# Output projection in seven products, convolution norm inside attention, and the second norm's rows transposed once

## The chip, the cores and the metric

The kernel runs on one core of a Trainium2 chip. The metric is the device time of one execution in microseconds. A core has TensorE (PE in the profile; matmuls and transposes, accumulating in PSUM), VectorE (DVE), ScalarE (ACT), GpSimd (POOL) and SyncE (SP, which here only issues transfers). Each engine runs its own list of instructions in order and waits for the others through semaphores. PEld is the loading of weights into PE, which runs beside the matmuls.

## What is computed

One layer of a block over 1024 tokens of width 1024, in float32, cut to what matters here:

```
h = rms_norm(x, norm1_g);  a, gate, q, k, v = split(h @ w_in)
conv = silu(layer_norm(depthwise_conv31(a * sigmoid(gate)) + dw_bias, conv_ln_g, conv_ln_b))
attn = neighbourhood_attention(rms(q), rms(k), v, rpb)   # 8 heads, 8 x 16 windows on a 16 x 64 grid
x = x + concat(conv, attn) @ w_out                       # (1024 x 1024) @ (1024 x 1024)
h = rms_norm(x, norm2_g)
x = x + (silu(h @ w_gate) * (h @ w_up)) @ w_down         # width 2816
```

## The kernel before

Every float32 factor is split into a high part, rounded to the format in which PE is fast, and a low part, the remainder: ACT casts, then POOL or DVE subtracts (`split`, L103 to L108). A product is then three matmuls, high x high, high x low, low x high (`mac`, L110 to L114), each 128x128 by 128x512.

The program is written in the order in which each engine is to run; no scheduler moves it. Work beside the matmuls is put into a list, `woven`, of which `weave` runs one entry after each `mac` of a stage. Weights arrive in chunks of 128x1024: `want` lists them, `issue` has SP load the next one, `take` splits it, `take_parts` splits it in pieces. Long-lived and passing tiles of 128x1024 share one pool of 22 buffers (`G`), larger ones six of 128x4096 (`H`); PSUM has four banks `mm`, two `tp` and one double bank `cv`.

The stages: (1) the input projection, one tile of 24 matmuls after another (`project`, `glu_step`; each calls `step`), with the convolution's 31 taps on DVE, ACT and POOL behind it (DVE L319, POOL L345 into `pa`). (2) Attention, a loop over i to 33, one iteration for a block of queries and two heads: scores s (PE L615), exponentials (DVE L628 subtracts the maximum, ACT L630), a reciprocal (DVE L635) and a scaling on POOL (L637), six transposes p on PE (L646), copies (L651), and the product o with v (L662); iterations 16 to 31 have 384 columns, earlier ones 288. The position biases `tab` and the windows of v, `vw`, are loaded by SP. (3) The output projection: `proj` adds eight row blocks of `w_out` to one tile of 128 tokens and 512 columns, `pj` for the first half of the columns, `pk` for the second, and `resid` (L775) adds the input. Among these matmuls stand the convolution's layer norm (`conv_stats`: four transposes y, L728, statistics on DVE, L735, root on ACT, scaling) and its SiLU (`conv_silu`: four transposes z, L761). (4) Row norms (`norm2`, `norm2_out`, L867) and the left factors of the gate and up projection. That projection is already one of seven products of halves: A11, A12, A22 and four sums of halves, S1 to S4, as left factors. `t2_one` transposes the normed rows of the first four token tiles (8 groups of four transposes, L994); `s_T` transposes the sums and A22 (five operands, 20 groups, L963), after `s_sum` has formed them on the untransposed rows (L944). The right factors are halves of `w_gate` and `w_up` and four sums of them, formed by DVE (`t_sums`, L893), for 22 blocks of columns i; `prep` splits the next one. (5) The down projection, which the change leaves alone.

## Time and profile before

| | us |
|---|---|
| median of 3 runs | 1063.14 (1063.02 to 1063.66) |
| the profiled execution | 1064.03 |
| its span in the trace | 1062.2 |
| PE busy | 1045.4 (98%) |
| DVE busy | 699.8 (66%) |
| ACT busy | 443.7 (42%) |
| POOL busy | 397.3 (37%) |

The span is from the first to the last instruction of the profiled execution. Shares of busy time are means over stages that differ. Matmuls overlap in the pipeline, so that their pitch, from one start to the next, says what one costs, and not the length of a row.

### The profile page before, as it was taken

The numbers are of one execution on the slowest core, as the hardware profiler recorded it, in microseconds if no ns is written. First come the engines' busy times: TensorE is split into PE (matmuls) and PEld (weight loads), VectorE is DVE, ScalarE is ACT, GpSimd is POOL, SyncE is SP. The second block draws the span as 40 slices with busy tenths as digits, with TensorE's granted clock in tenths as the row PEclk, the third lists the DMA queues.
The fourth block names the chain that finished last, engine by engine and source line by source line (L and its number), as shares of the span: only waits on it lengthen the run. The fifth ranks groups of instructions, "written<-read, shape, count | busy, mean of one in ns | idle before, by whom it ended". The sixth has DMA issues, their size and how long they took to land.

```text
span 1062.2 us, 13969 instructions
## 1 busy us (share of the span) xinstructions
PE 1045.4 (98%) x5068; PEld 847.3 (80%) x5068; DVE 699.8 (66%) x1072; ACT 443.7 (42%) x874; POOL 397.3 (37%) x308
## 2 busy tenths in 40 slices
PE   7999999999999999999999999999999999999997
PEld 5788888776667888788888888888888888888886
DVE  6768998966765247666565564564655567858883
ACT  6456346626776334532323223332233344433441
POOL 0126568823542301444554544545454200002310
PEclk9999999999999999999999999999999999999999
DMA  9416681245504412032322222232132597634641
GB/s 333 164 47 225 217 257 36 75 161 154 165 34 161 136 80 99 21 129 77 136 91 104 109 99 95 104 129 100 70 131 78 194 322 276 209 99 132 205 127 43
DMA packets 68244, 144.05 MB, mean 136 GB/s; under 512 B 12496, under 2 KB 21200, under 8 KB 67536
## 3 DMA queue, kind: packets, MB, share of 16 engines
q1 hardware_dynamic: 66336, 139.95, 38.3%
q10 hardware_dynamic: 1840, 3.22, 0.9%
q8 instruction: 40, 0.66, 0.3%
q14 instruction: 28, 0.23, 0.1%
HBM read 103.99 MB, written 44.76 MB: 140 GB/s over the span
## 4 chain that ended last, share of the span: by engine, by line
PE 94%; DMA 2%; DVE 1%; ACT 1%; POOL 1%; issue 0%; SPq 0%; POOLq 0%; ACTq 0%
PE B L112 6%; PE B L114 6%; PE B L113 6%; PE A L112 4%; PE D L112 4%; PE D L114 4%; PE A L114 4%; PE D L113 4%; PE A L113 4%; PE z L113 3%; PE z L112 3%; PE z L114 3%; PE gl L114 3%; PE gl L112 3%; PE gl L113 3%; PE o L662 2%
## 5 line engine op out<-in xcount | busy, mean ns | idle before, releaser
L319 DVE SCALAR_TENSOR_TENSOR cv<-u,par,cv 128x1009 f32<-128x1009 f32 (+14 forms) x85 | 108.5, 1276 | 1.9
L345 POOL TENSOR_TENSOR pa<-pa,pr 128x1022 f32<-128x1022 f32 (+10 forms) x31 | 74.2, 2392 | 35.5 <-ACT pr L344 26.5
L104 ACT CAST op<-sr 128x512 fp32r<-128x512 f32 x77 | 47.7, 619 | 52.1 <-PE B2d L114 26.3
L108 DVE TENSOR_TENSOR op<-sr,op 128x512 fp32r<-128x512 f32 x77 | 57.1, 742 | 16.1 <-ACT op L104 16.0
L1037 DVE TENSOR_TENSOR g<-B,g 128x512 f32<-128x512 f32 x22 | 15.2, 691 | 79.0 <-PE B L114 79.0
L1209 POOL TENSOR_TENSOR ou<-ou,resm 128x512 f32<-128x512 f32 x8 | 12.2, 1530 | 144.0 <-DMA resm<-xd 142.1
L1046 ACT ACTIVATE D<-D 128x512 f32<-128x512 f32 x22 | 12.8, 582 | 113.1 <-DVE D L1045 113.1
L1032 DVE TENSOR_TENSOR u<-B,g 128x512 f32<-128x512 f32 x22 | 15.2, 691 | 62.1 <-PE B L114 62.1
L104 ACT CAST op<-wd 128x512 fp32r<-128x512 f32 x66 | 40.9, 620 | 30.7 <-DVE wd L1124 18.4
L637 POOL TENSOR_SCALAR e<-e,rs 128x288 f32<-128x288 f32 (+1 forms) x64 | 34.1, 545 | 50.2 <-DVE rs L635 42.9
L108 DVE TENSOR_TENSOR op<-wd,op 128x512 fp32r<-128x512 f32 x66 | 50.4, 764 | 1.8
L893 DVE TENSOR_TENSOR ts<-gu,ts 128x512 f32<-128x512 f32 x44 | 51.0, 1159 | 0.8
L1035 ACT ACTIVATE A<-A 128x512 f32<-128x512 f32 x20 | 11.6, 582 | 76.3 <-PE A L114 76.3
L630 ACT ACTIVATE e<-e,mx 128x288 f32<-128x288 f32 (+1 forms) x64 | 36.2, 569 | 2.0 <-DVE mx L628 2.0
L628 DVE CUSTOM_DVE_ANT_0 e<-s,tab 128x288 f32<-128x288 f32 (+1 forms) x64 | 30.1, 505 | 8.1 <-PE s L615 8.0
L344 ACT ACTIVATE pr<-u,par 128x1022 f32<-128x1022 f32 (+10 forms) x31 | 34.2, 1135 | 1.2 <-ACT vs L405 1.2
L893 DVE TENSOR_TENSOR ts<-gu 128x512 f32<-128x512 f32 x22 | 34.1, 1551 | 0.0
L646 PEld LDWEIGHTS p<-ident,e 128*96 128x96 f32 (+1 forms) x192 | 20.1, 133 | 15.2 <-issue 10.5
L944 POOL TENSOR_TENSOR xn<-xn,xn 128x512 f32<-128x512 f32 x4 | 6.9, 1732 | 57.3 <-DVE sn L944 57.3
L646 PE MATMUL p<-ident,e 128*96 128x128 f32 (+1 forms) x192 | 27.6, 280 | 0.7 <-DVE pT L651 0.6
L662 PE MATMUL o<-pT,vw 96*64 96x128 f32 (+1 forms) x384 | 28.0, 281 | 0.0
L615 PE MATMUL s<-kT,qT 64*128 64x288 f32 (+1 forms) x128 | 26.7, 495 | 0.0
(1039 smaller groups left out, 3449.6 us busy)
## 6 DMA issues: line engine op xcount, KB each, us to landing
gu<-in_gu SPq DMA_DIRECT2D x44, 512.0 KB
sr<-sd SPq DMA_DIRECT2D x77, 256.0 KB
sd<-sd SPq DMA_DIRECT2D x22, 512.0 KB
wd<-in_wd SPq DMA_DIRECT2D x44, 256.0 KB
sd<-g SPq DMA_DIRECT2D x33, 256.0 KB
x<-in_x SPq DMA_DIRECT2D x16, 512.0 KB
xd<-x SPq DMA_DIRECT2D x8, 512.0 KB
resm<-xd SPq DMA_DIRECT2D x16, 256.0 KB
```

Source lines behind the costliest of these rows:

```text
L104: act.copy(hi, src)
L108: eng.tensor_tensor(*[w[..., sl] for w in (lo, src, hi.bitcast(F32))], OP.subtract)
L112: pe.matmul(acc, lh, rh, start=start, stop=False, skip_group_check=True)
L113: pe.matmul(acc, lh, rl, start=False, stop=False, skip_group_check=True)
L114: pe.matmul(acc, ll, rh, start=False, stop=stop, skip_group_check=True)
L319: dve.scalar_tensor_tensor(acc[:, o], uc[:, i], dwk[:, c, t:t + 1], acc[:, o], OP.mult, OP.add)
L344: act.activation(pr[:, o], uc[:, i], AF.Copy, scale=dwk[:, c, t:t + 1])
L345: pool.tensor_tensor(pa[:, o], pa[:, o], pr[:, o], OP.add)
L630: act.activation(e[:, hh], e[:, hh], AF.Exp, bias=mx, scale=-1.0, accum_out=rs[:, hh:hh + 1])
L646: pe.transpose(pt[:m, g * P:(g + 1) * P], es[i][:, hh, g * m:(g + 1) * m], ident)
L662: pe.matmul(os_[s_][hh * HD:(hh + 1) * HD, hp], vw[cb, rh + g][:, c:c + HD], pTs[i][:, g, hh], start=g == 0, stop=g == 2)
L893: dve.tensor_tensor(o, l, r, OP.subtract)
```

## The change

Five edits go together.

1. The output projection becomes seven products of halves. Tokens are halved (tiles 0 to 3 and 4 to 7), so are the rows of `w_out` (attention, convolution) and its columns. Products n1, n7, n4, n6, n5, n2, n3 run in this order, each over four token tiles `cb` and four row blocks `c`; n7 goes on in the banks of n1, n5 in those of n6. The left factors are `a11` (attention of the second token half), the convolution's two halves `A22` and `A12`, and Q1 to Q4, sums kept in the tiles `diff` and `rowf`, which DVE forms as results leave PSUM (`evac_lo`, `conv_diff`) and ACT and POOL split (`q_split`). The right factors are B11, B21, B22 and four block sums P1 to P4. `read` and `put` add each result to the input's rows.
2. Block sums of weights are made in DRAM: P1 to P4 of `w_out` (`w4`) and of the first four blocks of gate and up (`g4`). SP copies a block to DRAM, then POOL issues a transfer that adds another to it. P2 is made from P1, P4 from P2. The eight steps of `g4`, a megabyte each, lie at eight of the first eleven calls of `step`; the sixteen of `w4`, half a megabyte each, at the later projections and inside attention.
3. The convolution's norm moves into attention: transposes, statistics and an ACT copy at every third iteration to i = 24, the reciprocal root by a few small DVE operations instead of ACT's root, the scaling of two tiles in each of i = 28 to 31, from SBUF to SBUF. Four weight chunks instead of two are split inside attention, one piece per iteration from i = 13 on.
4. The second norm's rows are transposed once (`turn`, 16 groups of four); the sums S1 to S4 are formed on the transposed tiles and split without PE.
5. The first four gate and up blocks take their sums from DRAM; their splits all run on POOL, and their products come in another order. Signs of the sums change for all blocks, with additions and subtractions swapped at the results.

The core of the diff:

```diff
+    def sum_steps(w, parts):
+        h = P // parts
+
+        def put_(n, m, i):
+            return lambda: nc.sync.dma_start(pw[w, n][i * h:i * h + h], block(w, m)[i * h:i * h + h])
+
+        def add(n, m, i):
+            return lambda: pool.dma_start(pw[w, n][i * h:i * h + h], block(w, m)[i * h:i * h + h], accum_op=OP.add,
+                                          max_dma_last_dim=2048)
+        both = range(parts)
+        head = [put_(n, "B12", i) for n in ("P1", "P3") for i in both]
+        head += [add(n, m, i) for n, m in (("P1", "B11"), ("P3", "B22")) for i in both]
+        tail = [f(n, m, i) for n, l, r in (("P2", "P1", "B22"), ("P4", "P2", "B21"))
+                for f, m in ((put_, l), (add, r)) for i in both]
+        head.insert(7, tail.pop(0)) if parts == 2 else None
+        return head + tail
...
+    for n in ("B11", "P3", "P4", "P2", "P1", "B21", "B22"):
+        for j in range(2):
+            want(block("w4", n)[64 * j:64 * j + 64].rearrange("r (h e) -> (r h) e", h=2), f"{n}{j}", wq_dst(n, j))
...
+        if n_steps[0] in (1, 2, 4, 5, 6, 8, 9, 11):
+            gate_steps.pop(0)()
...
+        if t % 2:
+            aside_sum()
...
     def value(t):
+        if t % 2 == 0 or t > 4:
+            aside_sum()
...
-        act.copy(at[cb][0][:, :, rh], os_[s_])
-
-    def evac_lo(s_, cs=slice(0, 4)):
+            if not rowf:
+                rowf.extend(G(f"rf{j}").rearrange("p (c b q) -> p c b q", c=2, b=4) for j in range(2))
+            for j in range(2):
+                act.copy(rowf[j][:, :, cb], os_[s_][:, 2 * j:2 * j + 2])
+        else:
+            a11[cb] = [w.rearrange("p (c q) -> p c q", c=4) for w in lr(G(f"a11{cb}", F32R))]
+            act.copy(a11[cb][0], os_[s_])
...
+            dve.tensor_tensor(diff[j][:, :, cb], os_[s_][:, cs], rowf[j][:, :, cb], OP.subtract)
...
+    LHS = {"n7": "Q3", "n4": "A22", "n6": "Q2", "n5": "Q1", "n2": "A12", "n3": "Q4"}
+    RHS = {"n1": "B11", "n7": "P3", "n4": "P4", "n6": "P2", "n5": "P1", "n2": "B21", "n3": "B22"}
+    CB = (0, 3, 1, 2)
...
+            mac(acc, lhs(p, c, cb), [w[:, o + c * 512:o + c * 512 + 512] for o in (0, 2048)],
+                start and c == 0, c == 3)
...
+    def conv_norm(t):
+        y = conv_T(t)
+        st6 = SM(f"bs{t}", 6)
         dve.bn_stats(st6, y)
-        dve.bn_aggr(mv, st6)
-        act.activation(sd, mv[:, 1:2], AF.Sqrt, bias=eps)
-        cs[t] = y, mv, sd
-        if 1 <= t <= 4:
-            conv_scale(t - 1)
-        if t >= 4:
-            conv_scale(t)
-
-    def conv_scale(t):
-        y, mv, sd = cs.pop(t)
-        r = SM(f"br{t}", 1)
-        dve.reciprocal(r, sd)
+        dve.bn_aggr(mvs[:, t], st6)
         if t % 2 == 0:
-            xx = G(f"xh{t}")
-            xh.extend([xx[:, :512], xx[:, 512:]])
-        if t >= 6:
-            dve.tensor_scalar(xh[t], y, mv[:, 0:1], r, op0=OP.subtract, op1=OP.mult)
-        else:
-            nb = SM(f"bb{t}", 1)
-            dve.scalar_tensor_tensor(nb, mv[:, 0:1], -1.0, r, OP.mult, OP.mult)
-            act.activation(xh[t], y, AF.Identity, bias=nb, scale=r)
+            xh.extend(lr(G(f"xh{t}")))
+        act.copy(xh[t], y)
...
+    def conv_scale(t, eng):
+        eng.tensor_scalar(xh[t], xh[t], mvs[:, t, 0:1], rc[:, t:t + 1], op0=OP.subtract, op1=OP.mult)
...
+    def read(p, cb):
+        acc = pb[cb]
+        if p == "n1":
+            put(4 + cb, 0, acc)
+            put(4 + cb, 1, acc, OP.subtract)
+        elif p == "n7":
+            put(cb, 1, acc, OP.subtract)
+            put(cb, 0, acc)
+        elif p in ("n4", "n6"):
+            put(cb, 0, acc, OP.add if p == "n4" else OP.subtract)
+        elif p == "n5":
+            put(cb, 1, acc)
+            put(4 + cb, 1, acc)
+            norm2(cb)
+        elif p == "n2":
+            put(4 + cb, 0, acc)
+        else:
+            put(4 + cb, 1, acc)
+            norm2(4 + cb)
...
+        if i in (13, 17, 21, 25):
+            take_parts(jobs, more=i < 21)
+        for _ in range({2: 1, 4: 1, 5: 2, 18: 1, 21: 1}.get(i, 0)):
+            aside_sum()
...
+        if i % 3 == 0 and i < 27:
+            conv_norm(i // 3 - 1)
+        if i == 25:
+            root = rsqrt(rc, mvs[:, :, 1], "rc")
+        if 25 <= i < 28:
+            next(root)
+        if 28 <= i < 32:
+            conv_scale(2 * i - 56, dve)
+            conv_scale(2 * i - 55, dve)
...
+        if jobs:
...
+    products = [(i, p) for k in (0, 2) for p in ("m1", "m2") for i in (k, k + 1)]
+    products += [(i, p) for k in (0, 2) for p in SRC for i in (k, k + 1)]
+    products += [(i, p) for i in range(4, FB) for p in ORDER]
...
+    def turn(t, j):
+        if not h2:
+            h2.extend(H(f"h2{w}", F32R).rearrange("p (k s) -> p k s", s=512) for w in range(2))
+        pt = (tp, mm)[j](f"t2{t}{j}")
+        for i in range(4):
+            kb = 4 * j + i
+            pe.transpose(pt[:, i * P:(i + 1) * P], xn[t][:, kb * P:(kb + 1) * P], ident)
...
+            act.copy(hi, p3)
+            act.copy(w, pt)
+            rest.append(lambda: dve.tensor_tensor(lo, p3, hi.bitcast(F32), OP.subtract))
...
+    def group(p, cbs=CB):
+        for cb in cbs:
+            more = p in ("n7", "n5")
+            if not more:
+                pb[cb] = mm(f"{p}{cb}")
+            proj(p, cb, pb[cb], start=not more)
+            read(p, cb)
...
+    weaves(12, s0=lambda: (weigh(31), evac_hi(7), evac_lo(7)), s1=QS("Q3", diff, 0, pool), s2=lambda: tails.pop()(), s3=lambda: read("n1", 0),
+           s4=QS("Q3", diff, 1, pool), s6=C(0, 1), s10=take)
+    group("n1", CB[1:])
...
+    weaves(16, s1=C(0, 2), s5=take, s9=C(0, 3), s13=QS("Q2", diff, 0, pool))
+    group("n7")
...
+           s7=U(1, 0), s8=U(1, 1), s9=[lo2, lo2, prep], s10=[U(2, 0), take], s11=U(2, 1), s12=[lo2, lo2], s13=prep)
+    group("n2")
+    weaves(16, s3=prep, s7=prep, s9=N(4), s12=U(4, 0), s13=[U(4, 1), N(7)], s15=SS(0, 1, 2))
+    group("n3")
```

Three places show where instructions moved. First POOL, where the taps of the convolution end (`pa3`) and attention begins (`e0`, `e1`: the scaling of exponentials). Before:

```order
L345 TENSOR_TENSOR pa3_1620<-pa3_1620,pr327_1959 128x1012
L637 TENSOR_SCALAR e0_2066<-e0_2066,rs0_2067 128x288 x2
L637 TENSOR_SCALAR e1_2109<-e1_2109,rs1_2110 128x288 x2
L637 TENSOR_SCALAR e2_2146<-e2_2146,rs2_2147 128x288 x2
L637 TENSOR_SCALAR e3_2171<-e3_2171,rs3_2172 128x288 x2
```

and in the change:

```order
L212 DMA w4P1_65<-in_w4 256x512
L372 TENSOR_TENSOR pa3_1638<-pa3_1638,pr326_1940 128x1013
L372 TENSOR_TENSOR pa3_1638<-pa3_1638,pr327_1981 128x1012
L212 DMA w4P3_67<-in_w4 256x512 x2
L676 TENSOR_SCALAR e0_2091<-e0_2091,rs0_2092 128x288 x2
L212 DMA w4P2_66<-in_w4 256x512
L676 TENSOR_SCALAR e1_2135<-e1_2135,rs1_2136 128x288 x2
L676 TENSOR_SCALAR e2_2173<-e2_2173,rs2_2174 128x288 x2
L212 DMA w4P2_66<-in_w4 256x512
```

Adding transfers for P1, P3 and P2 now stand between the taps and between the scalings; POOL runs them in this order.

Then DVE at iterations 27 to 29 of attention (`e28`, `e29`: maximum subtracted; `pT`: the copy of a transposed tile; `mx` the read of its maximum). Before:

```order
L651 COPY pT25_2972<-p25_2965 128x3x128
L674 TENSOR_TENSOR at11_2824<-o5_2851,at10_2823 128x2x128
L635 RECIPROCAL rs27_2975<-rs27_2975 128x2
L628 ISA e28_3007,mx280_3009<-s280_2991,tab11_2356 128x384
L628 ISA mx280_3009 128x1
L628 ISA e28_3007,mx281_3012<-s281_2993,tab11_2356 128x384
L628 ISA mx281_3012 128x1
L651 COPY pT26_3005<-p26_2998 128x3x128
L674 TENSOR_TENSOR at11_2824<-o5_2851,at10_2823 128x2x128
L635 RECIPROCAL rs28_3008<-rs28_3008 128x2
```

and in the change:

```order
L726 TENSOR_TENSOR a111_3095<-o5_2968,a111_3095 128x256
L727 TENSOR_TENSOR df0_2512<-o5_2968,rf0_2337 128x2x128
L674 RECIPROCAL rs27_3116<-rs27_3116 128x2
L667 ISA e28_3155,mx280_3157<-s280_3139,tab11_2404 128x384
L667 ISA mx280_3157 128x1
L667 ISA e28_3155,mx281_3160<-s281_3141,tab11_2404 128x384
L667 ISA mx281_3160 128x1
L690 COPY pT26_3153<-p26_3146 128x3x128
L835 TENSOR_SCALAR xh0_2215<-xh0_2215,par_93 128x512 x2
L726 TENSOR_TENSOR a111_3095<-o5_2968,a111_3095 128x256
L727 TENSOR_TENSOR df1_2513<-o5_2968,rf1_2338 128x2x128
L674 RECIPROCAL rs28_3156<-rs28_3156 128x2
```

Between the copy of `pT26` and the next reciprocal, which POOL's scaling waits for, there now stand two scalings of convolution tiles (L835) and a second subtraction per evacuation (L727).

Last POOL at the end of attention. Before:

```order
L637 TENSOR_SCALAR e31_3110<-e31_3110,rs31_3111 128x384 x2
L108 TENSOR_TENSOR wo00_3190<-wo00r_2790,wo00_3190 128x256 x4
L108 TENSOR_TENSOR wo00_3190<-wo02r_3058,wo00_3190 128x256 x4
L108 TENSOR_TENSOR wo14_3576<-wo14r_3196,wo14_3576 128x1024
L108 TENSOR_TENSOR wo14_3576<-wo16r_3257,wo14_3576 128x1024
```

and in the change:

```order
L676 TENSOR_SCALAR e31_3260<-e31_3260,rs31_3261 128x384 x2
L118 TENSOR_TENSOR Q3_3369<-df0_2512,Q3_3369 128x1024
L118 TENSOR_TENSOR Q3_3369<-df1_2513,Q3_3369 128x1024
L118 TENSOR_TENSOR wP4_3421<-P40r_3278,wP4_3421 128x1024
L118 TENSOR_TENSOR wP4_3421<-P41r_3306,wP4_3421 128x1024
L118 TENSOR_TENSOR Q2_3510<-df0_2512,Q2_3510 128x1024
```

Weight chunks (`wP4`) now alternate with splits of operands (`Q3`, `Q2`), which need the last results of attention.

More of the change, by code (lines that the diff above doesn't have):

```diff
@@ L8 @@
 F32R = mybir.dt.float32r
+I32 = mybir.dt.int32
 AF = mybir.ActivationFunctionType
@@ L165, in part @@
                 raws.pop(i)
-                issue()
+                if more:
+                    issue()
         pos[1] += 1
@@ L959, in s_T @@
-        two = kb == 2
-        pt = cv("sp") if two else tp("sq")
-        for j in range(1 + two):
-            for t in range(4):
-                pe.transpose(pt[:, j * 512 + t * P:j * 512 + (t + 1) * P],
-                             s_rows(n, t)[:, (kb + j) * P:(kb + j + 1) * P], ident)
-        if two and n != "S4":
-            split(*[w[:, kb:kb + 2].rearrange("p k s -> p (k s)") for w in sop[n, "all"]], pt, (dve,))
-        else:
-            for j in range(1 + two):
-                split(sop[n][0][kb + j], sop[n][1][kb + j], lr(pt)[j] if two else pt, (dve,))
@@ L971, in s_weave @@
-    def s_weave(n):
-        skip = lambda: None
-        parts = [lambda kb=kb: s_T(n, kb) for kb in range(3)]
-        woven.extend([skip, skip, skip, skip, parts[0], parts[1], prep, parts[2]] if n == "S2" else
-                     [parts[0], skip, parts[1], skip, parts[2]])
+            split(sop[n][0][t], sop[n][1][t], s4[t // 2][:, t % 2], (eng,))
+            return
+        if n not in sop:
+            q = H(n, F32R).rearrange("p (w k s) -> p w k s", w=2, s=512)
+            sop[n] = [[q[:, h, i] for i in range(HK)] for h in range(2)]
+            sop[n, "all"] = [q[:, h] for h in range(2)]
@@ new lines, in build @@
+    group("n4")
+    weaves(16, s0=C(1, 2), s2=take, s5=C(1, 3), s7=QS("Q1", rowf, 1, pool), s10=take, s13=QS("Q4", diff, 0, pool))
+    group("n6")
+    weaves(16, s1=take, s3=QS("Q4", diff, 1, pool), s6=take, s9=N(0), s13=N(3))
+    group("n5")
+    while pos[0] < len(chunks):
+        issue()
+    for _ in range(3):
+        next_raw()
+    weaves(16, s0=take, s1=[N(1), U(0, 0)], s2=U(0, 1), s3=[lo2, lo2], s4=U(3, 0), s5=[U(3, 1), N(2)], s6=[lo2, lo2],
+           s7=U(1, 0), s8=U(1, 1), s9=[lo2, lo2, prep], s10=[U(2, 0), take], s11=U(2, 1), s12=[lo2, lo2], s13=prep)
```

400 lines of the change are left out of this document (221 added, 179 removed).

## The prediction

> **What bounds the kernel now.** I read the page first: the engines' shares, the granted clock, the chain that ended last.
>
> ```profile
> span 1062.2 us, 13969 instructions
> ...
> PE 1045.4 (98%) x5068; PEld 847.3 (80%) x5068; DVE 699.8 (66%) x1072; ACT 443.7 (42%) x874; POOL 397.3 (37%) x308
> ...
> PEclk9999999999999999999999999999999999999999
> ...
> GB/s 333 164 47 225 217 257 36 75 161 154 165 34 161 136 80 99 21 129 77 136 91 104 109 99 95 104 129 100 70 131 78 194 322 276 209 99 132 205 127 43
> ...
> PE 94%; DMA 2%; DVE 1%; ACT 1%; POOL 1%; issue 0%; SPq 0%; POOLq 0%; ACTq 0%
> ```
>
> TensorE is busy 98% of the span, is 94% of the chain that ended last, and never loses its clock. Then TensorE's waits, the longest and the one that concerns the second norm:
>
> ```profile
> PE z L112 <- ACT wk0h L104: 6.9, 1, 6.9
> ...
> PE t L994 <- DVE xn L867: 0.6, 1, 0.6
> ```
>
> Only the first is long, and the change does not touch the start. So an instruction taken off TensorE is worth its pitch, unless another engine in that stage becomes late. Last, the busy time of PE, PEld, DVE, ACT and POOL in the stages concerned, with clock, DMA share and GB/s behind them:
>
> ```profile
> 35.00:60.00 25.00, 25.00 (x119) 20.68 (x118) 20.62 (x38) 10.79 (x18) 2.52 (x2) 1.00 0.12 44
> ...
> 160.00:216.00 56.00, 54.91 (x257) 44.86 (x256) 50.80 (x58) 35.48 (x53) 48.51 (x22) 1.00 0.16 55
> ...
> 274.00:310.00 36.00, 36.00 (x325) 22.90 (x326) 27.39 (x94) 28.92 (x87) 22.14 (x37) 1.00 0.24 82
> ...
> 310.00:390.00 80.00, 79.95 (x419) 64.62 (x420) 34.86 (x74) 35.24 (x60) 17.40 (x16) 1.00 0.36 125
> 390.00:465.00 75.00, 73.90 (x376) 60.16 (x375) 51.62 (x75) 35.75 (x64) 23.11 (x17) 1.00 0.17 64
> ```
>
> The second half of attention is 274 to 310 us, the output projection and second norm lie in 310 to 465 us.
>
> **Part 1, matmuls removed.** The output projection has 8 token tiles x 2 column halves x 8 row blocks x 3 = 384 matmuls of 128x512; seven products of 4 x 4 x 3 make 336. That is 48 fewer. Their pitch, and what four transposes cost between them:
>
> ```profile
> 342.58 0.60 PE L761 MATMUL z<-ident,xh 128*128 128x128 f32 x4
> 342.93 0.47 PE L112 MATMUL pj<-wo,cm 128*128 128x512 f32 x1
> ...
> 344.17 0.39 PE L114 MATMUL pj<-wo,cm 128*128 128x512 f32 x1
> 344.40 0.60 PE L761 MATMUL z<-ident,xh 128*128 128x128 f32 x4
> ```
> ```profile
> 357.15 0.39 PE L112 MATMUL pj<-wo,at 128*128 128x512 f32 x1
> ...
> 358.51 0.39 PE L112 MATMUL pj<-wo,at 128*128 128x512 f32 x1
> ```
>
> From 357.15 to 358.51 are six matmuls: 0.227 us each (the 0.39 us is one pipelined instruction's length). 48 x 0.227 = 10.9 us off.
>
> **Part 2, transposes removed.** From 342.58 to 344.40 lie four transposes and six matmuls: 1.82 - 6 x 0.227 = 0.46 us for a group of four. Before, the second norm's rows are transposed in 8 groups and the five sums of their halves in 20; now the rows once, in 16, and the sums are formed behind it. 12 x 0.46 = 5.5 us off. The 8 groups of the convolution's norm leave the projection for attention at the same price: zero on TensorE. PE's sum is 1062.2 - 10.9 - 5.5 = 1045.8 us.
>
> **Part 3, what attention takes on.** Here PE is full and the other engines nearly are. One of the wide iterations:
>
> ```profile
> 301.71 0.92 PE L615 MATMUL s<-kT,qT 64*128 64x384 f32 x4
> ...
> 302.55 0.88 PE L646 MATMUL p<-ident,e 128*128 128x128 f32 x6
> ...
> 302.77 0.17 DVE L635 RECIPROCAL rs<-rs 128x2 f32<-128x2 f32 x1 [0.31 <-ACT e L630]
> 302.89 0.56 DVE L628 CUSTOM_DVE_ANT_0 e<-s,tab 128x384 f32<-128x384 f32 x1
> 303.11 1.14 POOL L637 TENSOR_SCALAR e<-e,rs 128x384 f32<-128x384 f32 x2 [1.32 <-DVE rs L635]
> ...
> 303.38 0.09 DVE L628 DVE_READ_ACCUMULATOR2_ANT mx<- 128x1 f32 x1
> ...
> 303.52 0.48 ACT L651 COPY pT<-p 128x384 f32<-128x384 f32 x1 [0.78 <-PE p L646]
> ...
> 303.90 0.62 ACT L630 ACTIVATE e<-e,mx 128x384 f32<-128x384 f32 x1
> ...
> 304.17 0.59 PE L615 MATMUL s<-kT,qT 64*128 64x384 f32 x2
> ```
>
> The period is 304.17 - 301.71 = 2.46 us, so 36 us are some 14.6 iterations. The pieces added to 274 to 310, by the nearest rows:
>
> ```profile
> L735 DVE BATCH_NORM_STATS2 bs<-y 128x6 f32<-128x512 f32 x8 | 5.6, 695 | 2.4 <-PE y L728 2.4
> ...
> L752 DVE TENSOR_SCALAR xh<-y,bm,br 128x512 f32<-128x512 f32 x2 | 1.6, 810 | 0.1
> L736 DVE BATCH_NORM_AGGREGATE bm<-bs 128x2 f32<-128x6 f32 x8 | 1.5, 182 | 0.3
> ```
> ```profile
> L669 ACT CAST at<-o 128x512 fp32r<-128x512 f32 x8 | 4.6, 569 | 0.0
> ...
> L104 ACT CAST wo<-wo04r 128x256 fp32r<-128x256 f32 x4 | 1.6, 391 | 0.0
> ```
>
> DVE: about four statistics at 0.695 + 0.182 = 0.88 (3.5 us) and eight scalings, which in the trace stand only with a PSUM source, 0.81 each (6.5): 27.4 + 3.5 + 6.5 = 37.4 us of work in 36. ACT: four copies at 0.57 (2.3), some six more weight casts at 0.39 (2.3): 28.9 + 4.6 = 33.5, 93% of the window. POOL has 14 us free for six more splits.
>
> The eight scalings lie in the last four iterations, two in each, 1.6 us where DVE has 2.46 x (1 - 27.4 / 36) = 0.6 free: 1.0 us short four times over, of which the last one to two may run out under the projection's first matmuls. That bounds this piece between 0, if a scaling from SBUF to SBUF costs half of the PSUM row, and 4 us; I take 1.5. [...]
>
> Elsewhere in attention, iterations where a statistic, a conv copy and an evacuation meet are over 2.46 us on one engine while the mean is under it; besides, long-lived tiles take buffers from the pool that the exponentials use, so that from the sixteenth iteration on several of them wait until TensorE has read the tile of two iterations earlier. The loop behind such a wait is two score passes (1.3 us by the rows above), the exponential of the second part and its sum (0.62 + some 0.2), the reciprocal 0.17, the scaling on POOL 1.14 and p 0.88: 4.3 us of the 4.92 of two iterations. A statistic (0.88) in between makes it 5.2, 0.3 too many. At most about a third of the 16 wide iterations meets one: 0 to 2 us; I take 1. Four of POOL's accumulating transfers are issued here too; no POOL transfer stands in the trace, and the cheapest row next to it is a scaling held up by one POOL operation, 0.58: 0 to 2 us; I take 0.5. Attention: +3.0 us, between 0 and 8.
>
> **Part 4, the projection and second norm.** Before loses 75.0 - 73.9 = 1.1 us in 390 to 465, of which 0.6 is the row above, transposes that wait for normed rows. These go with their code: -1.1. Now TensorE waits where the order of products runs into an operand: the second product needs the first difference split on POOL.
>
> ```profile
> L108 POOL TENSOR_TENSOR wo<-wo14r,wo 128x1024 fp32r<-128x1024 f32 x1 | 2.4, 2418 | 23.9 <-ACT wo L104 23.9
> ```
> ```profile
> L775 DVE TENSOR_TENSOR x<-pj,x 128x512 f32<-128x512 f32 x8 | 5.1, 685 | 11.3 <-PE pj L114 11.3
> ```
>
> POOL has some 18 splits of 2.42 (8 of operands, 10 of weights), 44 us, in the 76 that 336 matmuls take; DVE 36 additions at 0.69 (25) and about 31 for the convolution and norms. Neither fills the stage, but the second product is due 36 matmuls, two groups of transposes and one o after the first full column of the first, 36 x 0.227 + 1.4 = 9.5 us, and its operand is ready after the last evacuation and the convolution result that enters it (some 3.5 us of DVE and ACT rows at 0.4 to 0.7) and two splits of 2.42: 8.4 us. At the end, the last two normed rows come within a microsecond of their transposes. Between 0 (all in time) and 4 us (both late by one 2.4 us split); I take 1.5, near the 1.1 of before.
>
> **Part 5, sums in DRAM.** Sixteen megabytes more are copied or accumulated, 8 MB for gate and up beside the input projection and 8 MB for the output weights later. The cover is the rows above: the DMA engines are 12% busy in 35 to 60 us and 16% in 160 to 216. POOL is 10% busy in 35 to 60, so that it can stand at a wait there. The later points:
>
> ```profile
> 89.19 0.39 SPq L141 DMA_DIRECT2D ag13r<-in_ag  x1
> ```
> ```profile
> 111.28 1.03 ACT L104 CAST ag13h<-ag13r 128x1024 fp32r<-128x1024 f32 x1
> ```
> ```profile
> 208.97 7.29 POOL L345 TENSOR_TENSOR pa<-pa,pr 128x1014 f32<-128x1014 f32 x3 [0.52 <-ACT pr L344]
> 231.38 0.99 POOL L637 TENSOR_SCALAR e<-e,rs 128x288 f32<-128x288 f32 x2 [15.11 <-DVE rs L635]
> ```
>
> SP waits for an accumulation before it copies its result, with weight loads queued behind; a load is issued 111.28 - 89.19 = 22 us before its use. POOL issues four adds among the last products of the taps, then idles 15.1 us. I cost it at 0; without cover it is rival C. The first four gate and up blocks save DVE its sums; POOL splits them all, one per product of 12 matmuls (2.7 us), half of the 2.42 each: 0.
>
> **Sum.** 1045.8 - 1.1 + 3.0 + 1.5 = 1049.2 us span. The profiled execution took 1064.03, 1.8 more than its span and 0.9 more than the runs' median: 1049.2 + 1.8 - 0.9 = 1050.1, said as 1050 us, 1.2% faster.
>
> **The rivals.** *B, attention becomes bound by its helpers.* If every one of the 16 wide iterations pays the 0.3 us of the buffer loop or the short queue of ACT (93% full, in order), and the four scalings their full 4 us: 1050 - 3 + 16 x 0.3 + 4 = 1056; at 0.5 each, 1059. For it: DVE's 37.4 of 36. Against: the narrow first half has room, and spare work spills past 310. *C, slower: the accumulating transfers are slow.* SP's copy of the second gate sum stands behind the add of the first, issued two steps of 24 matmuls (2 x 24 x 0.227 = 10.9 us) earlier; with the loads' 22 us of lead TensorE waits once one add takes over 33 us per MB, and the chain of sums has two such places. The gain of 13 us is used up at 33 + 6.5, some 40 us per MB; at 45 it is 1050 + 2 x 12 = 1074. Against: the page's GB/s row has 333 in its first slice, by which a megabyte that is read and written takes some 6 us. [...] *D, nothing is late:* 1045.8 - 1.1 + 0.9 = 1045.6, if scalings are cheap and the queues absorb the peaks. That the change does less than it says is excluded by the program: PE's order has 48 matmuls and 48 transposes fewer.
>
> **How the numbers follow.** The forecast 0.57, D 0.15, B 0.2, C 0.08. The range that holds 8 in 10 reaches from below D to B's upper case: 1044 to 1060, with the tails and C outside. About 0.2% (2 us) can be told from no change; faster 0.88, same 0.04 (a B with more stalls, or C near its threshold), slower 0.08.
>
> **What would show it.** Matmuls of the projection at 0.227 us each and 336 of them; 64 transposes of normed rows; wide iterations at 2.46 us except the last four; the scaling's row near 0.4 or 0.8; PE's waits in 310 to 450 under 2 us in all; POOL and SP with no long idle time before weight loads. A period of 2.8 or more from the sixteenth iteration on makes B right; PE waiting for a cast of `ag` or `w` rows before 216 us, or for `vw`, makes C right.

## The result: 1.4% slower

The changed kernel took 1079.1 us (median of four runs, 1076.97 to 1080.49); the kernel before, on the same chip, 1063.4 (1063.02 to 1065.1). The ratio is 1.0143, with a 95% interval from 1.012 to 1.0166. The prediction was 1050, 1044 to 1060: wrong in sign, and outside its range.

**The profile after**, the page first:

```profile
span 1075.1 us, 13899 instructions
...
PE 1035.1 (96%) x4972; PEld 837.7 (78%) x4972; DVE 720.7 (67%) x1097; ACT 463.7 (43%) x911; POOL 454.6 (42%) x342
...
PEclk9999999999979999999999999999999999999999
...
PE 77%; DMA 5%; SPq 5%; issue 4%; DVE 4%; POOL 3%; ACT 2%; POOLq 0%; DVEq 0%; ACTq 0%
```

The 96 instructions are gone from TensorE (5068 to 4972) and its busy time fell by 10.3 us, yet the span grew by 12.9. TensorE's idle time rose from 1062.2 - 1045.4 = 16.8 us to 1075.1 - 1035.1 = 40.0. The chain that ended last, 94% PE before, is now only 77%, with 10% on transfers and on the queue that issues them, and one slice of the clock has a 7. The prediction had 1049.2 us of span, of which 1045.4 - 16.4 = 1029.0 busy and 20.2 idle. So it missed 19.8 us of idle time and 6.1 us by which TensorE was busy longer.

Where the idle time is, by TensorE's waits:

```profile
PE p L685 <- POOL e L676: 12.3, 2, 11.9
PE z L122 <- ACT wk0h L114: 5.9, 1, 5.9
PE p L685 <- DVE pT L690: 3.7, 6, 1.1
PE z L123 <- POOL pa L367: 3.4, 1, 3.4
PE z L123 <- POOL w02l L118: 1.9, 1, 1.9
PE t L1065 <- DVE xn L961: 1.2, 1, 1.2
PE B L124 <- POOL t0m L118: 1.1, 1, 1.1
PE B L122 <- DVE u L1183: 0.8, 1, 0.8
```

The second row stood there before (6.9). The rest falls into three places: attention (12.3 and 3.7), the input projection (3.4 and 1.9), and the second norm with the product that follows (1.2, 1.1, 0.8). The windows show the first two, and what the stalls do to the clock (busy PE, PEld, DVE, ACT, POOL; granted clock; DMA share; GB/s):

```profile
116.00:160.00 44.00, 38.08 (x159) 30.53 (x158) 35.65 (x32) 15.95 (x17) 30.59 (x14) 0.96 0.78 237
274.00:310.00 36.00, 27.09 (x236) 17.03 (x236) 20.43 (x74) 21.35 (x64) 17.09 (x28) 0.94 0.62 176
302.00:314.00 12.00, 1.14 (x10) 0.35 (x6) 0.68 (x4) 0.74 (x3) 0.26 (x1) 0.65 0.65 204
330.00:343.00 13.00, 11.37 (x97) 7.45 (x94) 12.70 (x42) 8.85 (x28) 6.89 (x13) 1.00 0.18 56
```
```profile
155.40:158.80 3.40, 3.40 (x8) 2.72 (x9) 3.26 (x5) 0.89 (x2) 3.40 (x2) 0.50 0.81 210
...
315.10:319.20 4.10, 4.10 (x22) 2.73 (x22) 1.85 (x7) 3.06 (x11) 2.48 (x5) 0.50 0.00 0
466.00:469.40 3.40, 3.40 (x10) 2.63 (x9) 3.29 (x4) 2.09 (x4) 3.40 (x3) 0.50 0.43 110
```

The last three rows are stretches behind or beside waits in which TensorE works at a granted clock of 0.50; matmuls of 128x512 start 0.43 us apart there (155.95 to 158.51 us, six of them) and 0.23 at the full clock (469.60 to 470.97, six).

From 302 to 314 us **every** engine stands: PE is busy 1.14 us of 12, DVE 0.68, ACT 0.74, POOL 0.26. ACT's timeline and SP's list say why:

```profile
300.16 0.59 ACT L816 COPY xh<-y 128x512 f32<-128x512 f32 x1
313.26 0.40 ACT L114 CAST wP<-P30r 128x256 fp32r<-128x256 f32 x1 [12.51 <-DMA P30r<-w4P]
313.57 0.47 ACT L690 COPY pT<-p 128x384 f32<-128x384 f32 x1
313.94 0.62 ACT L669 ACTIVATE e<-e,mx 128x384 f32<-128x384 f32 x1
```
```profile
278.40 2.34 SPq L627 DMA_DIRECT2D tab<-tf  x1
280.84 9.42 SPq L639 DMA_DIRECT2D vw<-vd  x4
290.35 9.76 SPq L151 DMA_DIRECT2D P30r<-w4P  x1
```

ACT came to the first cast of P3's chunk (`P30r`) and waited 12.51 us for the load; the copy and the exponential behind it, which do not use that chunk, waited too, and with them TensorE. SP issued the load only at 290.35, behind window loads (`vw`) and a bias table, and the issuing instruction alone lasted 9.76 us. The chain has the whole flight in one row:

```profile
290.35 22.83 DMA P30r<-w4P
```

The kernel before had the same kind of load, in the same crowd, and far more slack:

```profile
L141 SPq DMA_DIRECT2D wo00r<-in_wo x1: 6832/6832/6832, 277.2 to 277.2; - x1
```
```profile
L104 ACT CAST wo<-wo00r x1: 1034/1034/1034, 319.5 to 319.5; 128x1024 fp32r<-128x1024 f32 x1
```

Its first use was at 319.5, 42 us after the issue. It was slow too: of the sixteen completions that the trace records for it, twelve come at 286.9 to 287.7 and the last four at 294.2 to 295.9, 18.7 us after the issue. Apart from bursts, two to three tenths of the DMA engines are busy until 296 us, with the window loads (40 slices of 0.65 us from 274 to 300 us, in tenths):

```profile
DMA  3222231322222222579522224999222220000000
```

By moving two weight chunks into attention, the change put a deadline at 300.75 (313.26 - 12.51) on a load that went out later.

In the input projection SP is again at the start of it. SP between 64 and 82 us, and its long wait there:

```profile
66.91 4.62 SPq L512 DMA_DIRECT2D t<-in_rpb  x6
76.42 0.53 SPq L209 DMA_DIRECT2D g4P<-g4P  x1
```
```profile
SPq L209 <- DMA g4P<-in_g: 4.8, 1, 4.8
```

The copy that starts gate's P4 stands 4.8 us for the add that finishes P2, and everything behind it on SP is later. What reaches TensorE is the load of `w02r`; in the kernel before and after:

```profile
133.45 0.53 SPq L141 DMA_DIRECT2D w02r<-in_qkv  x1
```
```profile
142.94 0.53 SPq L151 DMA_DIRECT2D w02r<-in_qkv  x1
```

It goes out 9.5 us later, and TensorE waits 3.4 + 1.9 us soon after.

The theories at this point: **Q**, queues: loads leave SP too late, in attention (P3) and in the input projection (gate sums), and the idle time and the lost clock follow; the sums of work in the prediction are right. **R**, bandwidth: sixteen megabytes more of traffic slow every load, whatever the order. **S**, a part of Q: the gate sums alone cause the stalls before 160 us.

### The profile page after: what moved, and what is told of

The parts are those of the page before. It is cut to its first block, busy times and chain, and to the rows that moved or that the text cites. A ratio compares the mean times of both kernels' runs of the same rounds, so it can differ in the third digit from the quotient of the medians.

```text
span 1075.1 us, 13899 instructions
## 1 busy us (share of the span) xinstructions
PE 1035.1 (96%) x4972; PEld 837.7 (78%) x4972; DVE 720.7 (67%) x1097; ACT 463.7 (43%) x911; POOL 454.6 (42%) x342
## 4 chain that ended last, share of the span: by engine, by line
PE 77%; DMA 5%; SPq 5%; issue 4%; DVE 4%; POOL 3%; ACT 2%; POOLq 0%; DVEq 0%; ACTq 0%
PE B L124 5%; PE B L122 5%; PE B L123 5%; PE D L124 4%; PE D L122 4%; PE D L123 4%; PE A L124 3%; PE A L122 3%; PE A L123 3%; PE z L123 3%; PE z L122 3%; PE z L124 3%; PE n L122 2%; PE n L124 2%; PE n L123 2%
## 5 line engine op out<-in xcount | busy, mean ns | idle before, releaser
L1200 ACT ACTIVATE D<-D 128x512 f32<-128x512 f32 x22 | 12.8, 582 | 116.7 <-DVE D L1199 116.7
L685 PE MATMUL p<-ident,e 128*96 128x128 f32 (+1 forms) x192 | 29.1, 285 | 16.5 <-POOL e L676 12.3
L987 DVE TENSOR_TENSOR ts<-ts,gu 128x512 f32<-128x512 f32 x36 | 43.3, 1202 | 0.6
L873 DVE TENSOR_TENSOR x<-x,n 128x512 f32<-128x512 f32 x40 | 26.0, 680 | 14.3 <-PE n L124 13.1
L690 DVE COPY pT<-p 96x384 f32<-96x384 f32 (+1 forms) x32 | 17.7, 552 | 19.0 <-ACT pT L690 18.7
L987 DVE TENSOR_TENSOR ts<-gu 128x512 f32<-128x512 f32 x18 | 30.1, 1671 | 0.0
## 6 DMA issues: line engine op xcount, KB each, us to landing
g4P<-in_g POOLq DMA_DIRECT2D x4, 1024.0 KB, 12.5
```

The costliest lines, as they stand in the source:

```text
L685: pe.transpose(pt[:m, g * P:(g + 1) * P], es[i][:, hh, g * m:(g + 1) * m], ident)
L987: dve.tensor_tensor(lr(tsum[i, 1])[n - 3] if o is None else o, l, r, OP.add)
```

## The experiments

Each edit is against the changed kernel. Quoted expectations call the theories by these letters.

**1. P3's first load ahead of the windows**

```diff
+        if i == 6:
+            issue()
         if i in (6, 12):
             load_window(i // 6)
         if i in (13, 17, 21, 25):
-            take_parts(jobs, more=i < 21)
+            take_parts(jobs, more=i == 17)
```

(`more` has `take_parts` issue the next load too.)

> The changed kernel with one transfer moved: the load of the first chunk of P3 is issued by SP ahead of the window loads of iteration 6, instead of behind those of iteration 12. Theory Q (order of the queue): that load stood behind eight window loads which move only some 100 GB/s, landed at 313 us, and ACT, whose list is in order, stood at its cast with the exponentials behind it. Then ACT's wait of 12.5 us and TensorE's of 11.9 us go, the clock stays at full speed in attention, and the time is 1079 - 12 - 2 = about 1065 us. Rival E (attention's engines are simply full): the wait moves to the next iterations and the time stays above 1074 us.

Measured: 1069.37 us (1067.94 to 1070.02), ratio to before 1.0058 (1.0041 to 1.0074), 9.7 us less than the changed kernel. The windows from 250 to 320 us, of the changed kernel and of this one:

```profile
250.00:320.00 70.00, 55.98 (x495) 37.39 (x496) 40.27 (x149) 43.92 (x133) 32.39 (x57) 0.90 0.58 168
```
```profile
250.00:320.00 70.00, 64.67 (x570) 42.92 (x570) 48.74 (x177) 51.04 (x154) 37.05 (x64) 0.98 0.63 182
```

The same bytes in another order give TensorE 8.7 us more work in this stretch, at a clock of 0.98 instead of 0.90, and ACT has no wait for `P30r`. That is Q; R, whatever the order, would have kept the wait. The time is 4 us above the expected 1065: the stage still loses 5.3 us, and DVE now waits 4.9 us for the bias table `tab`, which stands behind P3's load.

**2. Without the sums for P4 of the output projection** (P2's weights stand in for P4's, so the result of that product is another; two copies and two adds in DRAM fall away)

```diff
-            want(block("w4", n)[64 * j:64 * j + 64].rearrange("r (h e) -> (r h) e", h=2), f"{n}{j}", wq_dst(n, j))
+            want(block("w4", "P2" if n == "P4" else n)[64 * j:64 * j + 64].rearrange("r (h e) -> (r h) e", h=2), f"{n}{j}", wq_dst(n, j))
...
-        for _ in range({2: 1, 4: 1, 5: 2, 18: 1, 21: 1}.get(i, 0)):
+        for _ in range({2: 1, 4: 1}.get(i, 0)):
```

> The changed kernel without the four steps in DRAM that make the block sum P4 (two copies by SP at iteration 5, two accumulating transfers by POOL at iterations 18 and 21); the product n4 then uses P2, so this part of the output is left out. All loads stay in their places. Theory Q: SP gains the 3 us of the two copies and some more from less traffic, so P3's chunk lands a few us earlier, but most of the wait stays: ACT's wait 5 to 10 us instead of 12.5, time 1070 to 1076 us. Rival R (the accumulating transfers hold the load up): the wait falls under 2 us and the time to about 1065 us.

Measured: 1071.56 us, one run.

```profile
ACT wP L114 <- DMA P30r<-w4P: 7.7, 1, 7.7
```

The wait shrank from 12.5 to 7.7 us and did not go. SP did not come to the load earlier (at 293.05, in the changed kernel at 290.35); the flight became shorter, 15.3 us instead of 22.8:

```profile
293.05 15.31 DMA P30r<-w4P
```

POOL's two adds for P4, issued at 288.94 and 298.81 in the changed kernel, are what no longer runs beside it. So R has a share, 4.8 us of the wait; the 7.7 us that are left go when the load leaves ahead of the window loads (experiment 1). Leaving this traffic out brought 7.5 us by this one run, and reordering 9.7.

**3. Without gate's sums** (B11 stands in for P1 to P4 of gate and up's first four blocks; all eight steps fall away)

```diff
-        if n_steps[0] in (1, 2, 4, 5, 6, 8, 9, 11):
+        if n_steps[0] in ():
             gate_steps.pop(0)()
...
-                src = block("g4", SRC[n])[64 * j:64 * j + 64].rearrange("(i r) (h e) -> (r h) i e", i=2, h=4)
+                src = block("g4", "B22" if SRC[n] == "B22" else "B11")[64 * j:64 * j + 64].rearrange("(i r) (h e) -> (r h) i e", i=2, h=4)
```

> The changed kernel without the eight steps in DRAM that make the gate and up block sums beside the input projection; the first four blocks then use block B11 in place of P1 to P4, so that part of the output is left out. Theory S (SP's wait): SP stood 4.9 us for the second accumulating transfer and some 4 us more at slowed bias loads, and SP has no slack because it issues without pause from 66 to 165 us, so the loads of w01 to w03 came 9.5 us late. Then TensorE's waits of 5.8 us between 145 and 157 us go, and w02's load is issued at about 133.5 us instead of 142.9; time about 1079 - 6 - 2 = 1071 us. Rival P: POOL's order of splits is the cause; the waits stay above 4 us.

Measured: 1069.21 us, one run. The window that lost 5.9 us is full, and `w02r` leaves as early as it did in the kernel before:

```profile
116.00:160.00 44.00, 44.00 (x196) 36.44 (x195) 41.16 (x41) 19.23 (x21) 32.60 (x15) 1.00 0.90 259
```
```profile
131.87 0.54 SPq L151 DMA_DIRECT2D w02r<-in_qkv  x1
```

So S holds: without the gate sums there is no stall from 116 to 160 us, and this one run is 9.9 us shorter than the changed kernel's median. ACT's wait for `P30r` is 12.4 us here: the two places are independent.

**4. Gate's steps closer together, and the early load of experiment 1**

```diff
-        if n_steps[0] in (1, 2, 4, 5, 6, 8, 9, 11):
+        if n_steps[0] in (1, 2, 4, 5, 6, 7, 9, 10):
```

> The early load of P3's chunk, and the gate sums' last four steps at steps 6, 7, 9 and 10 instead of 6, 8, 9 and 11, so that the second addition is issued before SP comes to the copy that waits for it. By theories Q and S: SP's wait of 4.9 us mostly goes, the loads of w01 to w03 come some 5 us earlier, TensorE waits 0 to 2 us there; time 1065 - 5 = about 1059 us, the first version faster than before. If the slowing of the bias loads by the last addition is what counts, most of the 5.8 us stay: about 1064 us.

Measured: 1064.55 us (1061.86 to 1066.6), ratio to before 1.0009 (1.0 to 1.0019): the expectation's second case, not its first. SP's copy no longer waits (it is issued at 71.36, as the transfer ahead of it is out), but `w02r` and TensorE gain little:

```profile
140.63 0.53 SPq L151 DMA_DIRECT2D w02r<-in_qkv  x1
```
```profile
PE z L123 <- POOL pa L367: 3.4, 1, 3.4
...
PE z L123 <- POOL w02l L118: 0.6, 1, 0.6
```
```profile
DVE e L667 <- DMA tab<-tf: 3.4, 1, 3.4
```

The wait was only part of it. With the wait gone `w02r` still leaves 7.2 us later than in the kernel before, and the transfers in flight are the suspect: in the changed kernel SP waits another 4.3 us after the last add, for its own small transfers for the bias table,

```profile
SPq L512 <- DMA tf<-neg: 4.3, 3, 2.1
```

and in this one, where the copy and the add for P4 still run beside them, it waits 2.0 us there and 3.0 us ahead of a weight load. And the early P3 load has pushed the bias table `tab` behind it, as in experiment 1: DVE waits 3.4 us for that. Here a load moved forward in SP's list moved another one back.

**5. Gate's P4 after the bias table, P3's load behind `tab`**

```diff
-        if n_steps[0] in (1, 2, 4, 5, 6, 8, 9, 11):
+        if n_steps[0] in (1, 2, 4, 5, 6, 7, 26, 29):
...
+        if i == 10:
+            issue()
```

(and `more=i == 17` as above, in all that follow)

> From the run with the early load and the tighter chain: the gate sums' last two steps (the copy for P4 and its addition) go to steps 26 and 29, behind the bias loads; P3's first chunk is issued at iteration 10, behind the last bias table instead of ahead of it. If SP's list and the traffic of the last addition delay w02 and w03, their loads come some 5 us earlier and TensorE's 4 us of waits for them go; the wait of 3.4 us for the table that was pushed back by P3's load goes too. Together 1064.5 - 4 - 3 = about 1058 us, faster than before by 0.5%. Rival: the last addition only moves its contention to the loads of the output weights; then TensorE waits elsewhere before 250 us and the time stays above 1062 us.

Measured: 1058.31 us (1056.53 to 1059.87), ratio 0.9955 (0.9939 to 0.997): faster than before, by 0.45%. Both waits of the input projection (for `pa` and `w02l`) are gone, so the copy and add for P4 beside the bias table were the rest of them; DVE still waits 2.8 us for `tab`, now behind the two copies for P4 of `w_out`.

**6. P4's copies late, and the scalings spread** (on top of 5: one scaling instead of two in each of the last four iterations, the other four among the first products)

```diff
-        for _ in range({2: 1, 4: 1, 5: 2, 18: 1, 21: 1}.get(i, 0)):
+        for _ in range({2: 1, 4: 1, 14: 2, 20: 1, 23: 1}.get(i, 0)):
...
-            conv_scale(2 * i - 56, dve)
-            conv_scale(2 * i - 55, dve)
+            conv_scale(i - 28, dve)
...
-           s4=QS("Q3", diff, 1, pool), s6=C(0, 1), s10=take)
+           s4=QS("Q3", diff, 1, pool), s6=C(0, 1), s7=CS(4), s9=CS(5), s10=take)
...
-    weaves(16, s1=C(0, 2), s5=take, s9=C(0, 3), s13=QS("Q2", diff, 0, pool))
+    weaves(16, s1=C(0, 2), s3=CS(6), s7=CS(7), s5=take, s9=C(0, 3), s13=QS("Q2", diff, 0, pool))
```

> As the run before, and the eight scalings of the convolution (0.53 us each in the changed kernel's trace) spread: four in iterations 28 to 31, four beside the first two products; the copies and additions for P4 of the output weights come later in attention (iterations 14, 20, 23). If DVE is the bound in 28 to 31 (two scalings there take 1.06 us where some 0.6 are free), 0.5 us come back in each of the four iterations: TensorE's waits for DVE's copies of p fall by 1.5 to 2 us and the time is about 1056 us. Rival: the exponentials wait for buffers that the transposes two iterations earlier free; then the waits stay and the time changes by less than 0.7 us.

Measured: 1069.18 us, ratio 1.005 (1.0037 to 1.0062), 10.9 us slower than experiment 5. This was an error of the edit, and it shows the mechanism a second time, on another engine:

```profile
POOL w4P L212 <- DMA w4P<-w4P: 12.8, 1, 12.8
```
```profile
PE p L685 <- POOL e L676: 14.4, 3, 12.9
```

The copies at i = 14 stand on SP behind four window loads; POOL reached the add that needs them and stood 12.8 us, with the scalings of exponentials behind it.

**7. The sums S4 later** (on top of 6: POOL's four additions and the splits of S4 moved back by one or two entries of the list for the second norm)

```diff
-        5: dict(s0=SS(1, 3), s1=SS(2, 3), s2=SS(0, 4, eng=pool), s3=SS(3, 4, eng=pool)),
-        6: dict(s0=SS(1, 4, eng=pool), s1=SS(2, 4, eng=pool), s3=SP("S3", 0)),
-        7: dict(s1=SP("S3", 3), s3=SP("S3", 1)),
-        8: dict(s1=SP("S3", 2)),
...
+        5: dict(s0=SS(1, 3), s1=SS(2, 3), s2=SS(0, 4, eng=pool)),
+        6: dict(s1=SS(3, 4, eng=pool), s3=SP("S3", 0)),
+        7: dict(s1=SP("S3", 3), s2=SS(1, 4, eng=pool), s3=SP("S3", 1)),
+        8: dict(s1=SP("S3", 2), s2=SS(2, 4, eng=pool)),
...
```

> As the run before, and the eight POOL operations that make the sum S4 (1.2 us each, 9.5 us in a row ahead of the splits of the next products) are spread over four products. If POOL's list is what delays the splits of the block sums at the start of gate and up, TensorE's waits of 2.7 us at that start fall to 1 us or less and the time is about 1054.5 us. Rival: the splits wait for the three load buffers and not for POOL; then no change (less than 0.5 us).

Measured: 1067.72 us, ratio 1.0037 (1.0024 to 1.0049), 1.5 us less than experiment 6, with ranges that touch. The waits of 1.1 us for `t0m` and 0.4 us for `t1m` are gone, which is as much.

**8. Experiments 6 and 7 without the error** (P4's copies back at i = 5)

> The version of 1058.3 us with the scalings spread and the S4 sums spread, but with P4's copies and additions left where they were: in the two runs before, the copies behind iteration 12's window loads were late, and POOL stood 12.9 us at its addition with the scalings of the exponentials behind it. If that alone made those two slow, their other two edits are worth what TensorE's waits showed: DVE's copies of p 5.3 to some 3 us, the start of gate and up 2.7 to 0.8 us; the time is 1058.3 - 2 - 1.8 = about 1054.5 us. If the spread scalings delay the first two products instead, it stays above 1057 us.

Measured: 1054.93 us (1053.64 to 1055.44), ratio 0.9917 (0.9904 to 0.9931), 3.4 us less than experiment 5. Of this 1.5 are the S4 sums by experiment 7. That the other 1.9 are the scalings isn't shown: from its first score to its last product o, attention takes 104.1 us in the traces of both (226.2 to 330.4 and 226.5 to 330.5). Two other waits changed there as well: DVE's for `tab` fell from 2.8 to 1.0 us, and ACT's for the second chunk of P3 grew from 1.4 to 2.5:

```profile
ACT wP L114 <- DMA P31r<-w4P: 2.5, 1, 2.5
```

**9 and 10. That wait from two sides**: P4's copies behind `tab` (9), or the splits of P3's second chunk later (10), each on top of 8.

```diff
 # 9
+        if i == 10:
+            aside_sum()
+            aside_sum()
+            issue()
...
+        for _ in range({2: 1, 4: 1, 20: 1, 23: 1}.get(i, 0)):
 # 10
-        if i in (13, 17, 21, 25):
+        if i in (13, 17, 21, 27):
```

> As the run before, and SP's two copies for P4 moved from ahead of the window loads of iteration 6 to behind the last bias table (iteration 10), the additions to iterations 20 and 23. In the version of 1058.3 us DVE waited 2.8 us for that table at 290 us. If the copies ahead of it, which themselves wait for the addition to P2, make it late, the wait falls under 1 us and the time by 1.5 to 2.5 us against the run before, to about 1052.5 us. If the eight window loads at 100 GB/s make it late, the wait stays and the time is the same within 0.7 us.

> The version of 1054.9 us with the splits of P3's second chunk started at iteration 27 instead of 25. There ACT again stood at a cast whose load had not landed (2.5 us at 307 us, the exponentials behind it). If that is the queue effect a second time, the wait goes and the time falls by 1.5 to 2.2 us to about 1053 us. If the four pieces then meet the scalings in iterations 28 to 31, TensorE's waits for p return there and the time stays.

Measured: 1055.53 us (1054.51 to 1055.93), ratio 0.9925 (0.9911 to 0.9938), for 9, and 1052.0 (1051.8 to 1054.65), ratio 0.9901 (0.9884 to 0.9917), for 10. Experiment 9 took the wait for `tab` from 1.0 to 0.6 us, and ACT's wait for the second chunk grew from 2.5 to 3.5 us: nothing gained, the delay only changed its owner. Experiment 10 moved the need instead of the load, and the wait is gone; its median is 2.9 us below experiment 8, though the intervals overlap.

**11. Both, with the splits at i = 22 and 28**

```diff
+        if i in (13, 17, 22, 28):
```

> The version with P4's copies behind the table (1055.5 us), with P3's two chunks split from iterations 22 and 28 on instead of 21 and 25. In that version DVE's wait for the table had gone, but ACT waited 3.5 us for P3's second chunk, which the copies pushed back. If these two are the same queue in another order, both waits are gone now and the time falls by 3 us to about 1052.5 us, the fastest so far; if late splits cost more than they save, it stays above 1054.5 us.

Measured: 1051.12 us (1050.5 to 1052.1), ratio 0.9885 (0.987 to 0.99). It leaves nothing of the computation out and is 1.15% faster than the kernel before; from experiment 10 its interval does not part it. Its page and the waits of TensorE that are left:

```profile
span 1048.7 us, 13899 instructions
...
PE 1027.9 (98%) x4972; PEld 833.7 (79%) x4972; DVE 719.4 (69%) x1097; ACT 463.8 (44%) x911; POOL 454.0 (43%) x342
```
```profile
PE p L685 <- POOL e L676: 1.5, 2, 0.9
PE p L685 <- DVE pT L690: 1.2, 4, 0.6
PE t L1068 <- DVE xn L964: 1.2, 1, 1.2
...
PE B L122 <- DVE u L1189: 0.8, 1, 0.8
```

The same 4972 instructions keep TensorE busy 1027.9 us here and 1035.1 in the changed kernel. Of these 7.2 us, which no row of waits shows, about 5.5 were the clock: in the three stretches at 0.50 above TensorE was busy 3.40 + 4.10 + 3.40 = 10.9 us and did half the work. The other 1.7 no row explains. No work has been taken out against the changed kernel, and the spans differ by 26.4 us.

The path from 1079.1 to 1051.1, by medians: P3's load early 9.7, gate's steps closer 4.8, P4 of gate late with P3's load behind the table 6.2, scalings and S4 spread 3.4, P4's copies and P3's splits later 3.8.

## Why the prediction was wrong, by its own steps

**Part 1 and Part 2, right.** 16.4 us were to come off TensorE's work. The last experiment has 1045.4 - 1027.9 = 17.5 us less busy time than the kernel before, with 48 + 48 instructions fewer, as forecast. In the changed kernel itself 10.3 of them can be seen; 5.5 of the other 7.2 went into the clock.

**Part 3, the step that failed.** The weight chunks moved into attention were costed by their casts (0.39 us each, so many per iteration) and by ACT's share of busy time, 93%. Of a moved step its transfer counts too, and the question for it was when SP would reach that load and when it would land. Both were in the trace of before: `wo00r`, behind the same window loads on SP's list, was issued at 277.2 and landed at 295.9. The change needs that load in iteration 21, right behind its exponentials, and in the trace of before these (ACT's 22nd pair) end at 287.8. An estimate from these times is 7 to 8 us late, with all of attention behind it: in the changed kernel ACT's copy and exponential stood behind the cast for its whole 12.51 us. Experiment 2, without P4's sums, waits 7.7 us; the measured 12.5 is that and the traffic of these sums. The prediction put this term at nothing: it named late casts of `ag`, `w` or `vw` as signs, and not P3.

The scalings of Part 3 came out between the two bounds, at 0.53 us:

```profile
L835 DVE TENSOR_SCALAR xh<-xh,par x8: 528/532/535, 333.9 to 342.2; 128x512 f32<-128x512 f32 x8
```

Before, from PSUM, the row was 0.81 (L752, 128x512). From SBUF the operation took two thirds of that; the half at which the lower bound was set was the author's assumption, and no run shows it. The cost was still there: from 330 to 343 us DVE is busy 12.70 of 13 and TensorE loses 13.00 - 11.37 = 1.6 us, where the term was 1.5. Attention as a whole in the last experiment, with the scalings spread, has 2.7 us of PE waits (1.5 + 1.2), for a term of +3.0.

**Part 4, the size was off.** The transposes and the next product wait 1.2 + 1.1 + 0.8 + 0.4 = 3.5 us (the last is a wait for `g`), for 1.5 taken between 0 and 4. The wait feared for the second product's operand did not come: no `n` matmul is among the waits. The late operands were those behind the norm.

**Part 5, the other step that failed, and rival C with it.** The sums in DRAM were costed at 0 because an add would have to take over 33 us per megabyte. It took far less (from issue to landing, median, for 1 MB and 0.5 MB):

```profile
g4P<-in_g POOLq DMA_DIRECT2D x4, 1024.0 KB, 12.5
w4P<-in_w POOLq DMA_DIRECT2D x8, 512.0 KB, 8.8
```

12.5 us is about twice the 6 us that the prediction drew from the rate, but far under 33, and the stall came all the same. The threshold was wrong: it added the 22 us lead of `ag13r`, one load, to the two steps, as though every load behind the wait had that lead, and POOL issued the add for P2 (64.92 us) only 6.7 us before SP came to the copy. The loads of `w02r` and after it had none to spare: in the kernel before, ACT already waits 0.7 us for `w02r`, and SP issues small transfers there without a pause. So the 4.8 us of waiting, the slowed transfers and the copies themselves came through as 9.5 us of delay. The same kind of wait, 14.7 us for the add ahead of the copy for P2, cost nothing, at a place where SP has slack: before, SP stands 28.0 us there for a tile of POOL (`neg`), in the changed kernel 16.7. The cover that was quoted, the DMA engines' 12%, says nothing on a queue: in 35 to 60 us the changed kernel loses nothing, with the share up from 0.12 to 0.83.

```profile
35.00:60.00 25.00, 25.00 (x120) 20.69 (x119) 20.98 (x38) 10.68 (x18) 4.55 (x4) 1.00 0.83 229
```

**The rivals and the chances.** C had the right mechanism for a part of the loss (a wait of SP with weight loads behind it), with 0.08, and its sign came: TensorE waits 1.9 us for `w02l` before 216 us. By experiment 3 that part is 9.9 of the 28.0 us between the changed kernel and the last experiment. C's condition, 40 us per MB, was not met, so that 1074 was near 1079 by luck of the sum. B's place was right (attention), but the load that arrived late was not its cause; what full engines cost in the changed kernel is at most some 4 us of waits (3.7 for DVE's copies, 0.4 for POOL). B's sign, a period of 2.8, is met even in the last experiment: its exponentials of i = 16 and 31 begin at 275.5 and 317.6, 2.81 us apart on average, where 2.46 was forecast. Of these 5.2 us at most 2.7 are TensorE's waits and 1.4 three groups of the convolution's transposes; the rest no row explains. A case "a moved load is late" was missing from the list, and with it most of the chance on the slower side. The term that the sum left out besides is the clock: the stall of 12 us cost 12 us and then 4.1 us at half rate.

What the prediction got right is the sum of work. Its span of 1049.2 us is near the 1048.7 of the last experiment, where the transfers leave in an order that meets their uses. In part that is luck: TensorE is busy 1.1 us less there than summed and idle 0.6 more, and scalings and S4 sums stand elsewhere than in the kernel that was forecast.

## What to carry to other kernels

When a step moves to an earlier stage, look up the load that feeds it: its place in the issuing engine's list, the landing time in the trace of before, and what stands behind the first instruction that waits for it on an engine that works in order. The busy share of the DMA engines said nothing on this here; the lists of SP and POOL did. A copy or a load inserted there delayed what stood behind it (`w02r` left 9.5 us later, and DVE waited 3.4 us for `tab` in experiment 4), so that each should be put behind the next transfer that has a deadline. Count a stall of TensorE as longer than it is: here 12 us cost about two more, for the clock.

## What was not expected of the hardware

- **The clock fell during a stall and stayed low after it.** TensorE stops at about 303.1 us; the granted clock is 0.50 from 305.5 to 319.2, though matmuls start again at 315.1, so that about 2 us of work are lost behind the stall (0.5 x 4.1). The fall comes 2.4 us after the last matmul, the release 4.1 us after the first. The other two stretches at 0.50, from 155.4 and from 466.0 us, last 3.4 us each. What sets these times no run here shows.
- **Some issues were slow in themselves.** The load of P3 took SP 9.76 us to issue at 290.35, the one for `P41r` 0.32 us at 324.34. Loads issued right behind four window loads took 6.83 us (`wo00r`, before), 2.71 (`P31r`, experiment 1) and 5.53 (`P31r`, experiment 11). What holds the instruction no run here shows.
- **Window loads moved about 100 GB/s.** From 275 to 280 us in the changed kernel, where SP issued nothing but these and one bias table, the DMA share was 0.25 and the rate 103 GB/s:

```profile
275.00:280.00 5.00, 4.70 (x47) 3.18 (x46) 3.83 (x17) 4.29 (x14) 2.67 (x5) 1.00 0.25 103
```

  A load issued behind them landed in two parts, as `wo00r` did before: of the sixteen completions of `P30r` twelve come at 305.0 to 306.3 us and the last four at 311.4 to 313.2. That these four wait for the window loads fits the times and isn't shown; no other layout of the windows was run.
- **Left open:** why an add of a megabyte takes 12.5 us, with a rate of 229 GB/s in the stretch of the first two.
